# Second block's attention: the score product with the keys' low part over all 128 rows of the array

## The chip, the cores and the metric

The kernel runs on one core of a Trainium2 chip. Its engines are TensorE (PE, matrix products; its weight loader is shown apart as PEld), VectorE (DVE), ScalarE (ACT), GpSimd (POOL) and SyncE (SP, which issues most DMAs). The metric is the device time of one execution in microseconds, as the median of several runs.

## The reference, cut to what matters

The reference is a transformer of two blocks over 256 tokens of width 1024, in 32-bit floats. The first block (forgetting attention beside a convolution, cross attention to a memory, a mixture of experts) is not touched. The second block mixes a gated recurrence with a sparse attention (`nsa_mixer`), then follow a feed-forward layer and a per-layer embedding. In that attention, 16 query heads share 4 heads of keys and values (each key head serves 4 query heads, head width 64). It has a compressed branch, a branch over selected blocks and a window branch; at 256 tokens the last two see all earlier tokens:

```python
s = jnp.einsum('bgrqd,bgqkd->bgrqk', qr, kg)
o_sel = jnp.einsum('bgrqk,bgqkd->bgrqd', masked_softmax(s, m_sel), vg)
...
s = jnp.einsum('bgrqd,bgkd->bgrqk', qr, kwb)
o_win = jnp.einsum('bgrqk,bgkd->bgrqd', masked_softmax(s, m_win), vwb)
```

`qr` are the rotated queries, `kg` and `kwb` the rotated keys of the two branches. What is computed for both is the causal softmax of the scores, times the values.

## The kernel before

The kernel keeps its precision by splitting 32-bit numbers into a high part in the rounded type F32R and the low part that is left over. A product of two numbers is then made of high x high, high x low and low x high. The projections do this with three products for each 128 channels (`dense_nat`, `dense_T`); the weights' parts are made on ACT and DVE (`wsplit`, lines 182 and 183, tiles `wh` and `wl`) from chunks that SP loads ahead.

In the second block's attention a head has only 64 channels, half of the array's 128 rows. The kernel uses the other half for the low parts. Of the rotated queries (`qr`), a head's high part lies in its half of the partitions (lower half for even heads, upper for odd ones) and its low part in the other half. The rotated keys' high part (`kh`) and low part (`kl`) lie in both halves: ACT and DVE write one, POOL copies the other (lines 1461 and 1462). One product of `qr` with `kh` over all 128 rows so gives high x high and low x high at once.

Function `att` walks over the 16 heads in 18 steps. In a step stand the scores of a head, the transposes of the head before, and the products with the values of the one before that. The scores of a head are made in two tiles, one for each half of the queries (`hf`): the first with 2 x 128 columns (both branches, the first 128 keys), the second with 2 x 256. So there are 32 score tiles, 16 of 256 columns and 16 of 512. A tile is the sum of three products in one bank of PSUM: `qr` with `kh` (written `tr<-kh,qr` in the rows below, moving operand first), `qr` with `kl` (`tr<-kl,qr`), and the causal mask, an identity times a table of zeros and large negative numbers on the last 128 keys of each branch (`tr<-cnr,idr`, always 256 columns). Then come, for the softmax (`exps`), a maximum on DVE (line 318, `anm`) and two exponentials on ACT (line 322, `P`). Score tiles have two buffers (`tr`), so a tile's first product waits until ACT has read the tile before the last one.

PE takes its instructions in the order in which the scheduler of the language has put them. It mixes the attention's steps with the projections of the gates and the merge (`mm<-wh,xTh` and the like, 512 columns), so between the score tiles PE works on those, on transposes (`hp<-cs,P`, line 1505) and on the values' products (`po<-vt,PT`). All matmuls but the transposes are recorded under line 193, the helper `mm`; the rows are told apart by their tiles. The same instruction stands as LDWEIGHTS on PEld and as MATMUL on PE. `64*128` in a row means 64 rows and 128 columns of the array in use, and `128x512` the tile that is written. Another place with 64 rows is the compressed branch (`po<-VB,cPT`, 256 columns, in runs of four).

Of the kernel before, what the change touches and what calls it, by code (L numbers as in the profile page):

```python
# [9 lines left out]
F32R = mybir.dt.float32r  # L10
# [6 lines left out]
S = 256  # L17
D = 1024
EPS = 1e-6
NEG = -1e30  # L20
CAP = 32
# [17 lines left out]
def _consts():  # L39
# [20 lines left out]
    for L in LEVELS:  # L60
        b, r = p // L, p % L
        # columns in the blocks' right halves only
        m = (b[:, None] == b[None, :]) & (r[:, None] < max(L // 2, 1))
        lv.append(m[:, r >= L // 2])
# [71 lines left out]
class B:  # L136
# [31 lines left out]
    def wsplit(self, raw, kc, n):  # L168
        """F32R parts of a raw chunk: lists of per-k [128, n] views."""
# [25 lines left out]
    def dense_nat(self, xT, w, K, c0, n, evac, halves=2, ring=None):  # L195
        """[tok, n] products for columns c0..c0+n of w; evac(half, psum)."""
# [17 lines left out]
    def dense_T(self, xT, w, K, c0, n, starts, evac, cuts=(4, 4)):  # L214
        """[feature, tok] products for the 128-column windows `starts` of
        columns c0..c0+n of w; evac(i, psum [128, 256])."""
# [18 lines left out]
    def sq(self, src, acc, junk=None):  # L235
        """acc [128, 1] <- sum(src^2) / D over the free axis of [128, 512]."""
        return self.nc.scalar.activation(self.junk() if junk is None else junk, src, AF.Square, scale=1.0 / 32, accum_out=acc)

    def rfin(self, acc, r, eps=EPS):
        """r [128, 1] <- 1/sqrt(mean + eps) from the two sums of sq()."""  # L240
        ms = self.sm.tile([128, 1], F32, name="ms", bufs=4)
        self.nc.vector.tensor_scalar(ms, acc[:, 0:1], acc[:, 1:2], eps, op0=OP.add, op1=OP.add)
        return self.nc.gpsimd.tensor_tensor(r, ms, self.mhalf, op=OP.pow)

    def split_out(self, ps, hv, lv, g=None):
        """psum -> F32R parts, times a per-partition gain."""
# [6 lines left out]
    def parts(self, pool, C=8, tag=None):  # L253
        """Tiles for transposed F32R parts; k -> [128, S] of chunk k."""
# [5 lines left out]
    def norm_T(self, x, gk, out, n=D):  # L260
        """x: natural halves [128, n] -> x*g as [chan, tok] F32R parts."""
# [15 lines left out]
    def scaled(self, out, x, r, engines):  # L277
        """out <- x * r by halves of the columns; r: [128, 1]."""
# [9 lines left out]
    def tr_parts(self, nat, out, g=None, pool=None):  # L288
        """natural halves [128, D] -> transposed F32R parts."""
# [11 lines left out]
    # Sigmoids and the like go by way of tanh, which shares a table with exp.  # L301
    def sigmoid(self, out, x, hb=0.0):
        """out <- sigmoid(x + 2 hb)"""
# [3 lines left out]
    def silu2(self, out, x, t=None):  # L307
        """out <- 2 silu(x); t: scratch, if out may not be it."""
# [5 lines left out]
    def exps(self, sc, P, n, nm, sm, r=None):  # L314
        """sc: [128, heads, n] psum, times r; P <- exp(sc - max), sm <- row sums."""
# [10 lines left out]
    def build(self, upto=99):  # L326
        tc, nc, A = self.tc, self.nc, self.A
        with ExitStack() as ctx:
# [18 lines left out]
            # sums of squares and factors of the norms over X, by half  # L347
# [19 lines left out]
    def setup(self):  # L367
        """Constants that nothing waits for at the start."""
# [4 lines left out]
        # softmax over the two rows of logits: first row's share, and the rest  # L373
# [10 lines left out]
        # lb + (1 - lb) sigmoid(x) = lb' + lm' tanh(x / 2)  # L384
# [3 lines left out]
    def block1(self):  # L388
        tc, nc, A = self.tc, self.nc, self.A
        V = nc.vector  # L390
        with tc.tile_pool(name="sm1", bufs=1) as self.sm, tc.tile_pool(name="b1", bufs=1) as b1, \
# [28 lines left out]
            # conv gate and value, forget logits  # L420
# [22 lines left out]
            # depthwise causal conv  # L443
# [18 lines left out]
            # log forget gates and their running sum  # L462
# [11 lines left out]
            # q, k, v. The heads of a pair have their channels in different halves of the  # L474
            # partitions; the other half carries the gates: one-hot rows against -c, c against ones.
# [42 lines left out]
            # forgetting attention  # L518
# [33 lines left out]
            # memory keys and values; in between, layernorm + swish on the conv path  # L552
# [68 lines left out]
            # memory cross attention; the scores take the norm's factors  # L621
# [49 lines left out]
            # the residual goes to psum, too, where the experts add to it  # L671
# [26 lines left out]
    def first_max(self, name, *vals):  # L698
        """For each (value [128, .., n], onehots, maximum): onehots of the first position
        of the maximum over the last axis. The steps of the values alternate."""  # L700
# [20 lines left out]
    def busy(self, t, x, n, pool=None):  # L721
        """Products of t and x that nobody reads: they hold TensorE's clock up over a wait."""
# [6 lines left out]
    def logits(self, c, pool, pl):  # L729
        """Routing products of columns c*512.. of x, before the norm's factor."""  # L730
# [13 lines left out]
    def route(self, pool, pl, x):  # L744
# [4 lines left out]
        with self.urgent():  # L749
# [6 lines left out]
            for h in range(2):  # L756
# [4 lines left out]
                # the two largest of every group; then the group's  # L761
# [11 lines left out]
            # place of each token in its expert's list, from 1  # L773
# [6 lines left out]
            with tc.issue_after(last.ins):  # L780
                # number of the tokens beyond their expert's first CAP
                V.tensor_scalar(sel, pos, float(CAP) + 0.5, None, op0=OP.is_gt)
                # gates
# [5 lines left out]
                # the experts' table, while the engine waits  # L789
# [14 lines left out]
    def beyond(self, pool):  # L804
        """Number of the tokens beyond their expert's first CAP."""
# [9 lines left out]
    def onehots(self, q, P):  # L815
        """Tokens (rows) to places in the lists of four experts."""
# [6 lines left out]
    def moe_plan(self):  # L823
        """The experts' weight chunks in the order of their use, by fours."""
# [11 lines left out]
    def more(self, n):  # L836
        """Opens a pool of n more places for the experts' chunks."""
# [5 lines left out]
    def mload(self):  # L843
        """Loads the next chunk: rows of 512 for each of the four experts, or the last norm's gains."""
# [24 lines left out]
    def moe(self):  # L869
        """Four experts at a time, each with its places in its own quarter of the  # L870
        array's columns and of psum's partitions."""
# [4 lines left out]
        with tc.tile_pool(name="smm", bufs=1) as self.sm, tc.tile_pool(name="mo", bufs=1, reuse_waits="tile") as mo:  # L876
            T = lambda n, name: mo.tile([128, n], F32, name=name)
            with tc.tile_pool(name="pbig", bufs=2, space=PSUM) as pbig, \
# [3 lines left out]
                def gather(q, n=4):  # L882
                    """Inputs of the places, by channel, and the norm's factors for them."""
# [19 lines left out]
                def products(a, n, ps):  # L903
                    """ps <- products of n row blocks a(k) with as many weight rows, by expert."""
# [7 lines left out]
                def gates_t(q):  # L912
                    """Gates of the places, by token."""
# [66 lines left out]
                # this block's last norm and the next one's first: X <- x * g, with  # L980
                # the sums of squares of x and x * g
# [18 lines left out]
            with self.urgent():  # L1000
                for h in range(2):
                    # 1 / rms(x) and 1 / rms(x * g), the latter with eps * rms(x)^2 for eps
# [10 lines left out]
    def overflow(self, y, T, psm):  # L1013
        """Tokens beyond the first CAP of an expert: every expert over all tokens."""
# [4 lines left out]
        def load(ap):  # L1019
            # a queue of its own: those of the other loads need not come to rest  # L1020
            nc.gpsimd.dma_start(raw, ap)
            return raw

        with tc.If(n > 0):
            # by halves of the tokens; most of these are other tiles' places
# [34 lines left out]
    def rope(self, x, hf, H):  # L1060
        """Rotates the first 16 of each 64 of x [128, H*64] in place."""
# [12 lines left out]
    def post(self, m, ps, h, c, gb, acc):  # L1074
        """m <- psum * gain, and the sum of squares of the psum."""
# [4 lines left out]
    def post_add(self, m, h, acc, eps=EPS):  # L1080
        """X[:, h] += m / rms."""
# [8 lines left out]
    def block2(self):  # L1090
        tc = self.tc
        with tc.tile_pool(name="eo", bufs=1) as eo:
            # the recurrence's outputs, later the per-layer embedding
# [4 lines left out]
    def mixer(self, on):  # L1098
# [4 lines left out]
        with tc.tile_pool(name="sm2", bufs=1) as self.sm, tc.tile_pool(name="b2", bufs=1) as b2, \  # L1103
# [8 lines left out]
            # the recurrence's values go first and take the norm's factors themselves  # L1112
# [16 lines left out]
            with tc.tile_pool(name="s5", bufs=2) as s5p, tc.tile_pool(name="ap", bufs=1) as ap, \  # L1129
# [16 lines left out]
                # gated merge of the two branches  # L1146
# [59 lines left out]
    def hgrn(self, uT, W, on, hv, hg, php, other):  # L1206
        """The gated linear recurrence, two heads at a time; channels on partitions."""
# [3 lines left out]
        for b in range(4):  # L1211
# [12 lines left out]
            # products to fill the chain's waits with  # L1224
# [5 lines left out]
    def heads(self, fo, qq, hv, on, h0, tile, php):  # L1230
        """Two heads of the recurrence.
        Each pair (t, s) falls in one block of a binary tree over time, with s
        in its left and t in its right half: keys carry the decay up to the
        half's end, queries that from the half's start, both products of
        factors <= 1 that grow from level to level."""
# [9 lines left out]
        def pairs(q, L):  # L1245
            """Pairs of the blocks of L; their queries are the right halves."""
# [17 lines left out]
        while m < 128:  # L1264
            # tot: products of f over blocks of m
# [30 lines left out]
        # the queries' factor dk**-0.5 / 2 comes in here, and the output gates' half  # L1296
# [12 lines left out]
    def nsa(self, uT, W, s4, b2):  # L1309
# [3 lines left out]
        # compressed keys and values: transposed, second half of the partitions one token ahead  # L1313
# [14 lines left out]
        def compress():  # L1328
            """Keys and values at once: theirs are the lower and the upper half of the array's columns."""
# [21 lines left out]
            # twice the gelu  # L1351
# [20 lines left out]
        # queries, transposed in pairs of heads  # L1372
# [23 lines left out]
        # gates  # L1396
# [8 lines left out]
        # compressed branch  # L1405
# [33 lines left out]
        # rotated keys of both branches as parts, in both halves of the partitions; values  # L1439
# [24 lines left out]
        # rotated queries: a head's high part in its half of the partitions, the low one in the other  # L1464
# [10 lines left out]
        def att(ap, pax):  # L1475
            """Selected and window branches: causal over all keys at this length.
            Scores of a step, the transposes of the one before and the values'
            products of the one before that follow each other."""
            acc, Ps, PTs = {}, {}, {}

            def scores(h):
# [7 lines left out]
                rr = slice(64 * j, 64 * j + 64)  # L1489
                for hf, kb, c0 in ((0, 128, 0), (1, 256, 128)):  # L1490
# [3 lines left out]
                    self.mm(sc, q[rr], kl[g // 2][rr, g % 2, :, :kb], False, False)  # L1494
# [44 lines left out]
    def ffn(self, e):  # L1539
# [3 lines left out]
        with tc.tile_pool(name="smf", bufs=1) as self.sm, tc.tile_pool(name="ff", bufs=1) as ff, \  # L1543
# [4 lines left out]
            with tc.tile_pool(name="py2", bufs=1, space=PSUM) as py, \  # L1548
                    tc.tile_pool(name="pmm", bufs=4, space=PSUM) as self.pmm:
                self.ptr, self.trtag = self.pmm, "mm"  # L1550
                # With v = x r, relu(v W)^2 is r^2 relu(x W)^2: the norm over its product has
# [116 lines left out]
```

## Time and profile before

| | |
|---|---|
| time, median of 3 runs | 1365.17 us (1363.2 to 1365.42) |
| span of the profiled execution, from first to last instruction | 1360.5 us |
| PE busy in the span | 1205.7 us (89%) |
| DVE, ACT, POOL busy | 603.3, 486.5, 130.8 us |
| instructions | 17824, of them 7122 matmuls |
| the attention's 32 score tiles | from 979 to 1082 us of the span |
| DMA over the span | 332.38 MB, mean 244 GB/s |

The span is one profiled execution; the runs' time is a little longer, as it holds what lies before the first and behind the last instruction. An engine's busy share is a mean over stages with different limits. In the middle of the span, 300 to 740 us, the experts' weights stream in and DMA is busy all the time; at both ends PE is. PE counts as busy from a matmul's recorded start to its modelled end, and matmuls overlap: what a matmul really takes is read from one start to the next.

### The profile page before, as it was taken

The page shows a single profiled execution, that of the slowest core. Times are in us where ns is not written, and L with a number is a line of the kernel's source. Part 1 is how long each engine was busy: PE and PEld are TensorE (multiplying, and loading weights), DVE is VectorE, ACT ScalarE, POOL GpSimd, SP SyncE. Part 2 cuts the span into 40 slices and gives each one's busy share as a digit, 9 for nine tenths or more (in the row PEclk, how much of TensorE's full clock was granted, in tenths as well). Part 3 has the DMA queues.
Part 4 walks back from the last instruction along what each step waited for, and adds up shares of the span by engine and source line. Part 5 has one row for each costly group of instructions (what it writes and reads, how often), then busy time and mean ns, then how long its engine had stood idle before and what let it go on. Part 6 is the DMA issues. An engine that isn't in the chain of part 4 may idle for free.

```text
span 1360.5 us, 17824 instructions
## 1 busy us (share of the span) xinstructions
PE 1205.7 (89%) x7122; PEld 839.1 (62%) x7122; DVE 603.3 (44%) x1024; ACT 486.5 (36%) x923; POOL 130.8 (10%) x171
## 2 busy tenths in 40 slices
PE   8889999989676766676768999999999999999997
PEld 7779888733121212020302898888778888989886
DVE  5896655510000000000002678575756666565565
ACT  5677654300000000000003543244655446554553
POOL 3876000000000000000000000014100000000000
PEclk9989999989686978786867999999999999999999
DMA  8333695899999999999999554553522245565651
GB/s 291 112 128 119 236 374 195 277 372 381 387 385 388 388 390 386 390 386 390 387 390 350 161 170 133 159 169 117 164 91 76 85 157 178 186 195 179 202 199 47
DMA packets 174328, 332.38 MB, mean 244 GB/s; under 512 B 6368, under 2 KB 20512, under 8 KB 174240
## 3 DMA queue, kind: packets, MB, share of 16 engines
q1 hardware_dynamic: 173680, 329.87, 68.6%
q8 instruction: 58, 0.95, 0.3%
q10 hardware_dynamic: 560, 1.31, 0.3%
q14 instruction: 30, 0.25, 0.1%
HBM read 330.11 MB, written 1.05 MB: 243 GB/s over the span
## 4 chain that ended last, share of the span: by engine, by line
PE 51%; DMA 23%; SPq 2%; ACT 1%; DVE 1%; issue 1%; DVEq 0%; POOLq 0%; ACTq 0%
PE mm L193 29%; DMA w<-w_gate_in 7%; DMA w<-w_up_in 7%; PE z L193 7%; DMA w<-w_down_in 6%; PE bg L193 5%; PE po L193 2%; PE hp L193 2%; DMA wl<-w_up_in 2%; PE tr L193 2%; SPq L859 2%; PE sp L193 2%; PE hp L1505 1%; PE sp L960 0%; DMA w<-w_in_in 0%
## 5 line engine op out<-in xcount | busy, mean ns | idle before, releaser
L183 DVE TENSOR_TENSOR wl<-w,wh 128x1024 fp32r<-128x1024 f32 (+2 forms) x228 | 278.5, 1236 | 160.2 <-ACT wh L182 158.9
L182 ACT CAST wh<-w 128x1024 fp32r<-128x1024 f32 (+2 forms) x228 | 235.6, 1044 | 202.5 <-PE mm L193 161.0
L193 PE MATMUL bg<-w,xs 128*32 128x512 f32 x888 | 160.6, 827 | 72.8 <-DMA w<-w_up_in 35.4
L193 PE MATMUL mm<-xTh,wl 128*128 128x256 f32 x688 | 196.4, 290 | 11.3 <-DVE wl L183 11.1
L193 PE MATMUL mm<-xTh,wh 128*128 128x256 f32 x688 | 190.6, 290 | 5.5 <-ACT wh L182 2.8
L193 PE MATMUL mm<-xTl,wh 128*128 128x256 f32 x688 | 194.0, 288 | 0.2 <-DVE xTl L251 0.2
L193 PE MATMUL mm<-wl,xTh 128*128 128x512 f32 (+1 forms) x440 | 173.1, 396 | 0.3 <-DVE wl L183 0.3
L193 PE MATMUL mm<-wh,xTh 128*128 128x512 f32 (+1 forms) x440 | 168.5, 401 | 4.0 <-ACT wh L182 1.3
L193 PE MATMUL mm<-wh,xTl 128*128 128x512 f32 (+1 forms) x440 | 170.4, 395 | 0.0
L958 DVE SCALAR_TENSOR_TENSOR sg<-bg,rsl,sg 128x512 f32<-128x512 f32 x8 | 6.0, 751 | 343.8 <-PE bg L193 343.8
L193 PEld LDWEIGHTS bg<-w,xs 128*32 128x32 f32 x888 | 23.6, 125 | 198.0 <-DMA w<-w_up_in 80.5
L193 PEld LDWEIGHTS mm<-xTh,wl 128*128 128x128 f32 x688 | 133.1, 194 | 14.5 <-DVE wl L183 13.8
L193 PEld LDWEIGHTS mm<-xTh,wh 128*128 128x128 f32 x688 | 130.2, 194 | 8.1 <-ACT wh L182 3.5
L193 PEld LDWEIGHTS mm<-xTl,wh 128*128 128x128 f32 x688 | 132.5, 194 | 0.8 <-DVE xTl L251 0.4
L193 PEld LDWEIGHTS mm<-wh,xTh 128*128 128x128 f32 x440 | 82.4, 189 | 21.7 <-ACT wh L182 1.8
L193 PEld LDWEIGHTS mm<-wl,xTh 128*128 128x128 f32 x440 | 83.2, 189 | 18.0 <-DVE wl L183 1.9
L193 PEld LDWEIGHTS mm<-wh,xTl 128*128 128x128 f32 x440 | 83.0, 189 | 17.9 <-issue 0.7
L193 PE MATMUL bg<-w,ht 128*32 128x512 f32 x456 | 65.2, 663 | 25.1 <-DMA w<-w_down_in 24.3
L461 POOL TENSOR_TENSOR zc<-zc,zt 128x256 f32<-128x256 f32 x60 | 63.1, 1053 | 17.2 <-ACT zt L458 12.5
L977 ACT COPY od<-bg 128x512 f32<-128x512 f32 x16 | 9.4, 585 | 139.5 <-PE bg L193 134.7
L962 ACT COPY ht<-sp 128x512 f32<-128x512 f32 x8 | 4.7, 585 | 152.2 <-PE sp L960 152.2
L1243 POOL MEMSET At<- 128x512 f32 x4 | 2.0, 525 | 565.2 <-PE bg L193 458.2
(410 smaller groups left out, 1586.6 us busy)
## 6 DMA issues: line engine op xcount, KB each, us to landing
w<-w_down_in SPq DMA_DIRECT2D x73, 1024.0 KB, 14.4
w<-w_up_in SPq DMA_DIRECT2D x68, 1024.0 KB, 14.0
w<-w_gate_in SPq DMA_DIRECT2D x59, 1024.0 KB, 14.3
w<-w_in_in SPq DMA_DIRECT2D x41, 1024.0 KB, 5.2
w<-w_mkv_in SPq DMA_DIRECT2D x8, 1024.0 KB, 5.1
w<-w_out_in SPq DMA_DIRECT2D x8, 1024.0 KB, 5.1
wh<-w_up_in SPq DMA_DIRECT2D x12, 512.0 KB, 11.6
wl<-w_up_in SPq DMA_DIRECT2D x12, 512.0 KB, 11.4
```

The lines of the kernel that those rows point to most:

```text
L182: self.nc.scalar.copy(hv, raw[:, j:j + g, :])
L183: self.nc.vector.tensor_tensor(lv, raw[:, j:j + g, :], hv.bitcast(F32), op=OP.subtract)
L193: return self.nc.tensor.matmul(out, lhsT, rhs, start=start, stop=stop, skip_group_check=True)
L461: nc.gpsimd.tensor_tensor(zi, zi, t, op=OP.add)
L859: self.nc.sync.dma_start(a, src[:, j * n:(j + 1) * n])
L958: V.scalar_tensor_tensor(sg, ps, rsl[q], sg, op0=OP.mult, op1=OP.mult)
L962: nc.scalar.copy(ht, tp)
L977: nc.scalar.copy(od[q, c], ps)
L1243: nc.gpsimd.memset(At, 0.0)
L1505: nc.tensor.transpose(pt[:, b * 128:(b + 1) * 128], P[:, br, b * 128:(b + 1) * 128], idn)
```

## The change

In `scores`, the product with the keys' low part takes the whole of `qr` and `kl` and no longer the head's half `rr` of the partitions. It sums over 128 rows instead of 64 and adds the product low x low, which was left out before. The diff also empties comments and docstrings; without those it is:

```diff
@@ scores(h)
                 P = Ps[h] = ap.tile([128, 2, 384], F32, name="P", bufs=2)
-                rr = slice(64 * j, 64 * j + 64)
                 for hf, kb, c0 in ((0, 128, 0), (1, 256, 128)):
                     sc = self.ptr.tile([128, 2, kb], F32, name="tr")
                     q = qr[g][:, h % 4, hf * 128:(hf + 1) * 128]
                     self.mm(sc, q, kh[g // 2][:, g % 2, :, :kb], True, False)
-                    self.mm(sc, q[rr], kl[g // 2][rr, g % 2, :, :kb], False, False)
+                    self.mm(sc, q, kl[g // 2][:, g % 2, :, :kb], False, False)
                     self.mm(sc[:, :, kb - 128:], self.idr,
                             self.cnr[:, None, :].to_broadcast([128, 2, 128]), False, True)
```

The instructions stand in the same order on every engine, with line numbers one less behind the removed line. Two waits change places on PE. At the first score tile the rows are these, with before marked by - and now by +:

```order
 L193 MATMUL mm<-wh,xTh_4931 128x512
 L193 MATMUL tr<-kh,qr 128x256 [waits DVE_49,PE_49,Pool_49]
-L193 MATMUL tr<-kl,qr 128x256
+L193 MATMUL tr<-kl,qr 128x256 [waits Pool_49]
 L193 MATMUL tr<-cnr,idr 128x256
 L193 MATMUL tr<-kh,qr 128x512
```

The first product with `kl` now waits for POOL's copy of the low parts; in the third score tile, of the second head, where this wait stood, it is gone.

## Rows read from the trace of the kernel before

**Rows 1.** The page's first part: busy us (share of the span) xinstructions of each engine.

```profile
PE 1205.7 (89%) x7122; PEld 839.1 (62%) x7122; DVE 603.3 (44%) x1024; ACT 486.5 (36%) x923; POOL 130.8 (10%) x171
```

**Rows 2.** Busy time by window: window, us, engines (xcount), granted clock, DMA share, GB/s.

```profile
978.00:1082.00 104.00, 104.00 (x572) 81.82 (x570) 58.46 (x114) 55.77 (x165) 0.00 (x0) 1.00 0.27 92
...
1146.00:1150.00 4.00, 3.53 (x17) 3.56 (x18) 3.30 (x8) 3.90 (x11) 0.00 (x0) 0.57 0.67 245
```

**Rows 3.** The chain that ended last, from 960 to 1110: shares by line.

```profile
by line: PE mm L193 57.9%; PE tr L193 18.6%; PE po L193 13.4%; PE hp L1505 7.0%; PE tr L296 1.6%; PE mm L296 1.2%; PE tr L1385 0.6%
```

**Rows 4.** Waits from 975 to 1100: us in total, times, longest us.

```profile
DVE anm L318 <- PE tr L193: 31.4, 23, 4.3
```

**Rows 5.** Groups of weight loads, 978 to 1082: busy us, mean ns | idle before.

```profile
L193 PEld LDWEIGHTS tr<-kh,qr 128*128 128x128 f32 x32 | 6.1, 190 | 0.3
...
L193 PEld LDWEIGHTS tr<-cnr,idr 128*128 128x128 f32 x32 | 6.0, 186 | 5.9 <-issue 3.9
L193 PEld LDWEIGHTS tr<-kl,qr 64*128 64x128 f32 x32 | 5.8, 183 | 6.8 <-issue 5.6
```

**Rows 6.** Timeline of PE, a 512-column tile: start us, us, what.

```profile
986.70 0.47 PE L193 MATMUL tr<-kh,qr 128*128 128x512 f32 x1
987.10 0.50 PE L193 MATMUL tr<-kl,qr 64*128 64x512 f32 x1
987.53 0.39 PE L193 MATMUL tr<-cnr,idr 128*128 128x256 f32 x1
987.75 0.38 PE L1505 MATMUL hp<-cs,P 128*128 128x128 f32 x2
987.89 0.48 PE L193 MATMUL mm<-wl,xTh 128*128 128x512 f32 x1
988.21 0.40 PE L193 MATMUL mm<-wh,xTl 128*128 128x512 f32 x1
988.44 0.39 PE L193 MATMUL mm<-wh,xTh 128*128 128x512 f32 x1
```

**Rows 7.** Timeline of PEld, the same place.

```profile
987.10 0.18 PEld L193 LDWEIGHTS tr<-kl,qr 64*128 64x128 f32 x1 [0.24 <-issue]
987.53 0.19 PEld L193 LDWEIGHTS tr<-cnr,idr 128*128 128x128 f32 x1 [0.24 <-issue]
...
987.97 0.19 PEld L193 LDWEIGHTS mm<-wh,xTl 128*128 128x128 f32 x1
```

**Rows 8.** Timeline of PE, 256-column tiles behind values' products and behind a projection's.

```profile
992.50 0.36 PE L193 MATMUL tr<-kh,qr 128*128 128x256 f32 x1
992.79 0.38 PE L193 MATMUL tr<-kl,qr 64*128 64x256 f32 x1
...
998.63 0.28 PE L193 MATMUL tr<-kh,qr 128*128 128x256 f32 x1
998.84 0.38 PE L193 MATMUL tr<-kl,qr 64*128 64x256 f32 x1
999.15 0.38 PE L193 MATMUL tr<-cnr,idr 128*128 128x256 f32 x1
```

**Rows 9.** Timeline of PE, a run of 256-column products with 128 rows.

```profile
1150.08 0.28 PE L193 MATMUL mm<-xTl,wh 128*128 128x256 f32 x1
1150.20 0.28 PE L193 MATMUL mm<-xTh,wh 128*128 128x256 f32 x1
```

**Rows 10.** Timeline of PEld, a run of four 64-row products and what follows.

```profile
917.60 0.73 PEld L193 LDWEIGHTS po<-VB,cPT 64*128 64x128 f32 x4 [0.36 <-issue]
918.66 0.19 PEld L193 LDWEIGHTS mm<-wh,xTl 128*128 128x128 f32 x1 [0.33 <-issue]
```

**Rows 11.** Instructions on `kl`: ns min/median/max, first and last start us.

```profile
L1462 POOL CAST kl<-kl x8: 393/402/1391, 947.8 to 957.7; 64x256 fp32r<-64x256 f32 x8
```

**Rows 12.** Timelines of ACT and PE: a tile's last exponential, and the tile that takes its buffer.

```profile
1034.72 0.38 ACT L322 ACTIVATE P<-tr,anm 128x128 f32<-128x128 f32 x1
...
1035.76 0.36 PE L193 MATMUL tr<-kh,qr 128*128 128x256 f32 x1
```

## The prediction

> **What bounds the kernel now.** I read three things in this order: which engine is busy where the change sits, whether that engine waits there, and what its idle moments are.
>
> The page's first part says that TensorE (PE) is busy 89% of the span [rows 1]. A share over the whole span says little about one stage, so the second view is the busy time in the 104 us from 978 to 1082, in which all 32 score tiles of the second block's attention lie: PE is counted busy for all 104.00 us, VectorE (DVE) for 58.46 and ScalarE (ACT) for 55.77, the granted clock is 1.00 (the 2.4 GHz level) and the DMA engines are 27% busy [rows 2]. The chain that ended last runs from 960 to 1110 through PE alone: the shares of its PE groups add up to 100% [rows 3]. The list of waits agrees: DVE waits 31.4 us for the scores [rows 4], and no line of that list is one of PE's matmuls. So a microsecond less on PE here is a microsecond less at the end, as long as ACT and DVE keep up.
>
> A PE that counts as busy is not a PE at full rate, because the ends of matmuls are modelled. The third view is therefore the weight loader (PEld). Before its 32 loads for the high-part product the loader sits idle 0.3 us in all; before the 32 loads for the low-part product, which have 64 rows, 6.8 us; before the 32 loads for the mask, which follow them, 5.9 us [rows 5]. These 12.7 us are what the change is about.
>
> One score tile shows it. The three products of a 512-column tile start at 986.70, 987.10 and 987.53, and the next work at 987.75 [rows 6]: intervals of 0.40, 0.43 and 0.22. Three 512-column products in a row that all use 128 rows start at 987.89, 988.21 and 988.44 [rows 6]: 0.32 for the one that follows short transposes, then 0.23. The loader says why. The load for the product at 988.21 begins at 987.97, 0.24 ahead, while the product before it runs. The loads for the low-part product and the mask begin at 987.10 and 987.53, the moment their own products are recorded to start, each with 0.24 of idle loader before it [rows 7]. They are not done ahead: one load and the emptying of the array lie bare, once going from 128 rows to 64 and once coming back.
>
> Elsewhere in the kernel there are 64-row products too, in runs of four. There the loader idles 0.36 us before the four loads, not between them, and 0.33 us before the first 128-row load behind them [rows 10]. So it is the change of the row count that costs, not the 64 rows as such, and what follows may be an ordinary projection product: the mask's own form is not needed for it.
>
> **The change part by part.**
>
> Removed: 32 times the step from 128 to 64 rows and 32 times the step back. Working by tiles, from start to start:
> - 512 columns (16 tiles): now 0.40 + 0.43 + 0.22 = 1.05. Afterwards 0.32 for the high part (behind short work, as [rows 6] has it), 0.23 for the low part, and for the mask's 256 columns what 256 columns take in a run of 128-row products, 0.12 [rows 9]: 0.67. Saved 0.38.
> - 256 columns behind a projection product (7 tiles): now 0.21 + 0.31 [rows 8] and 0.22 for the mask, 0.74. Afterwards three times 0.12, 0.36. Saved 0.38.
> - 256 columns behind short work (9 tiles): now 0.29 for the first interval [rows 8], 0.82 in all. Afterwards 0.21 (0.12, and 0.09 for the bare load, as 0.32 stands to 0.23), 0.12 and 0.12. Saved 0.37.
>
> Sum: 16 x 0.38 + 7 x 0.38 + 9 x 0.37 = 12.1 us. The cruder second way is the loader's idle time, 6.8 + 5.9 = 12.7 us [rows 5]. I take the middle, 12.4.
>
> Added: the low-part product sums over 64 more rows. Columns set how long a product streams, and these stay; a 128-row product of the same 512 columns takes 0.23 [rows 6], already in the sum. The weight loads stay 32 in number; those with 64 rows take no less time than those with 128 (5.8 us busy against 6.1 in [rows 5]). So the cost is zero, and the bound is that of the mask's interval, the one of which no row shows it behind a 128-row product of this kind: 0.12 at best, 0.22 if nothing changes there, that is 32 x 0.10 = 3.2 us less gain. I take 0.12, since [rows 10] puts the same gap before a plain product. A price below zero is excluded: the same columns still stream.
>
> Here the Trainium skill speaks against the change. Its page "TensorE: Matmul & The Clock Gate" (Part 3, The mechanism) says that a weight load overlaps with matmuls in flight "only when row_grp differs"; by that rule the new loads, which use all rows like the product before them, would lie as bare as now, and the sum would be zero. [rows 7] contradict it for this chip: a 128-row load runs 0.24 ahead under a 128-row product. By the trace the sum stays 12.4.
>
> Moved: nothing but one wait. Every engine's instructions stand in the same order; the first low-part product now waits for GpSimd (POOL), since it reads both copies of the keys' low part, and the third score tile, which did so before, no longer does. Behind the waiting instruction stands all of PE, but POOL's last copy of the low parts starts at 957.7 and the longest takes 1391 ns [rows 11]; the product comes behind 979, where the score tiles begin, some 20 us later. Cost nothing; cover 20 us. No DMA and no queue is passed.
>
> Where the time goes next: PE stays the last engine. A tile's buffer comes back from ACT, and the closest call that I found is the tile at 1035.76, whose buffer ACT had released at 1034.72 + 0.38 = 1035.10, 0.66 us ahead [rows 12]. A tile gains 0.38, and ACT's work is fed by PE and moves with it, so I count no new wait; the price if I am wrong in this crowded place (four tiles between 1030 and 1041) is 4 x 0.38 = 1.5 us. After the attention everything to the end hangs on PE and moves as a block. One loose term is there: from 1146 to 1150, behind the norm, the mean granted clock is 0.57 [rows 2], mostly the 1.2 GHz level. If the block lies differently against such a stretch, up to 1.5 us may come or go (4 us at about half rate, with PE in part waiting).
>
> The profile's span is 1360.5, the median of the runs 1365.17, so 4.7 us lie around the span. Span after: 1360.5 - 12.4 = 1348.1; time 1352.8.
>
> **The rivals.**
> - The mask's gap stays: its load is late for a reason of its own (a repeated operand, the same bank of PSUM) and not because rows change. For it: no row shows the mask behind a 128-row product of the new kind. Against it: [rows 10]. Only the idle before the low-part loads goes, 6.8: 1358.4.
> - The gain turns into waits for the softmax: PE reaches a tile whose buffer or exponentials aren't there. For it: 0.66 us at 1035.76 [rows 12]. Against it: ACT and DVE are busy little over half of the stretch [rows 2], and DVE waits for PE's scores [rows 4]. 1.5 us in the crowded place gives 1354.3; as much again elsewhere, 1355.8.
> - The change doesn't do what it says: the loads stay bare since all products of a tile share rows (the rule above), or they have to wait for something that isn't the row count. 1365.2. Against it: [rows 7, 10].
> - Slower: the 64-row product now runs beside its neighbours on the idle half of the array, and the change takes that away. Then 16 passes of 0.23 and 16 of 0.12 come on top, 5.6 us: 1370.8. It decides from the point at which a low-part product costs less than a full pass now. Against it: it costs 0.43 where a full pass takes 0.23 [rows 6]. The Trainium skill's page "TensorEngine Tiling (Array Packing)" (Overview, Theoretical Speedup) promises up to 2x for 64 rows; here no second 64-row product stands next to it, and the trace shows no gain.
>
> **How the numbers follow.** Forecast 1352.8, with waits of up to 1.5 us and the clock's 1.5 us in it: 82%. Mask's gap or more waits, 1356 to 1360: 10%. Nothing: 5%. Slower: 3%. The range: down to 1350.0 (12.7 gained, 1.5 of clock, 1 for the spread of runs, which lay between 1363.2 and 1365.4), up to 1357.5 (3.2 less for the mask and 1.5 of waits). About 0.2%, 2.7 us, is what a measurement can tell from no change: faster than 1362.4 takes the first two cases, 92%; within 5%; slower 3%.
>
> **What would show it.** In the trace after, the loader's idle time before the low-part and mask loads falls from 12.7 us to under 2; a 512-column tile's intervals read 0.32, 0.23 and 0.12; the 32 tiles end about 12 us earlier counted from the first; DVE waits less for the scores; no new wait of PE between 978 and 1090. If the mask's load still starts with its product, the first rival holds. If PE's list of waits names ACT, the second. I am wrong altogether if the low-part intervals stay at 0.43 and 0.31.

## The result, and the profile after

The changed kernel took 1348.26 us (median of 4 runs, 1347.07 to 1349.01), the kernel before, in the same session, 1364.49 (4 runs): ratio 0.9892, 95% interval 0.988 to 0.9904. It is faster by 16.2 us. The forecast was 1352.8, with a range down to 1350.0; the measured time lies 1.7 us below that end. The profiled execution has a span of 1347.3 and a time of 1348.96.

The page's first part: busy us (share of the span) xinstructions of each engine. It answers [rows 1].

```profile
PE 1192.2 (88%) x7122; PEld 838.0 (62%) x7122; DVE 603.8 (45%) x1024; ACT 486.3 (36%) x923; POOL 130.1 (10%) x171
```

PE does as many instructions and is busy 13.5 us less; ACT, DVE and POOL do what they did. Where it went is seen in the loader. The groups of weight loads of the score tiles (busy us, mean ns | idle time of the loader before them), which answer [rows 5]:

```profile
L193 PEld LDWEIGHTS tr<-kl,qr 128*128 128x128 f32 x32 | 6.1, 191 | 0.3
L193 PEld LDWEIGHTS tr<-kh,qr 128*128 128x128 f32 x32 | 6.1, 190 | 0.4
L193 PEld LDWEIGHTS tr<-cnr,idr 128*128 128x128 f32 x32 | 6.0, 188 | 0.7
```

The idle time before the low-part and the mask loads fell from 12.7 us to 1.0. The loads themselves last as long as before.

One 512-column tile on PE (start us, us, what), answering [rows 6]:

```profile
986.25 0.47 PE L193 MATMUL tr<-kh,qr 128*128 128x512 f32 x1
986.56 0.39 PE L193 MATMUL tr<-kl,qr 128*128 128x512 f32 x1
986.79 0.28 PE L193 MATMUL tr<-cnr,idr 128*128 128x256 f32 x1
986.91 0.38 PE L1504 MATMUL hp<-cs,P 128*128 128x128 f32 x2
```

and its loads on PEld, answering [rows 7]:

```profile
986.33 0.19 PEld L193 LDWEIGHTS tr<-kl,qr 128*128 128x128 f32 x1
986.56 0.19 PEld L193 LDWEIGHTS tr<-cnr,idr 128*128 128x128 f32 x1
```

From start to start it is 0.31, 0.23 and 0.12 where it was 0.40, 0.43 and 0.22. The loads now run 0.23 ahead of their products, under the product before. The two kinds of 256-column tiles, behind values' products and behind a projection's, answer [rows 8]:

```profile
991.65 0.36 PE L193 MATMUL tr<-kh,qr 128*128 128x256 f32 x1
991.86 0.28 PE L193 MATMUL tr<-kl,qr 128*128 128x256 f32 x1
991.97 0.28 PE L193 MATMUL tr<-cnr,idr 128*128 128x256 f32 x1
...
996.99 0.28 PE L193 MATMUL tr<-kh,qr 128*128 128x256 f32 x1
997.11 0.28 PE L193 MATMUL tr<-kl,qr 128*128 128x256 f32 x1
997.23 0.28 PE L193 MATMUL tr<-cnr,idr 128*128 128x256 f32 x1
```

Summed over all 32 tiles, from the first product's start to that of the instruction behind the mask, the tiles take 17.03 us where they took 29.51: 12.48 less. The whole attention, from the first score product to the last product with the values, went from 110.3 us (979.0 to 1089.3) to 97.8 (979.7 to 1077.5).

Nothing took the place of what was removed. The list of PE's waits from 960 to 1100 is empty, the chain in that stretch still runs through PE alone, and DVE waits less for the scores than in [rows 4] (us in total, times, longest):

```profile
DVE anm L318 <- PE tr L193: 20.1, 15, 3.9
```

### The profile page after: what moved, and what is told of

Same layout as the page of the kernel before. It is cut to its first block, busy times and chain, and to the rows that moved or that the text cites. A ratio compares the mean times of both kernels' runs of the same rounds, so it can differ in the third digit from the quotient of the medians.

```text
span 1347.3 us, 17824 instructions
## 1 busy us (share of the span) xinstructions
PE 1192.2 (88%) x7122; PEld 838.0 (62%) x7122; DVE 603.8 (45%) x1024; ACT 486.3 (36%) x923; POOL 130.1 (10%) x171
## 4 chain that ended last, share of the span: by engine, by line
PE 51%; DMA 24%; SPq 2%; DVE 1%; ACT 1%; issue 1%; DVEq 0%; POOLq 0%; ACTq 0%
PE mm L193 29%; DMA w<-w_up_in 8%; DMA w<-w_down_in 8%; PE z L193 7%; DMA w<-w_gate_in 6%; PE bg L193 5%; PE po L193 3%; PE hp L193 3%; SPq L859 2%; DMA wl<-w_up_in 1%; PE sp L193 1%; PE tr L193 1%; PE hp L1504 1%; PE sp L960 0%; DVE sg L958 0%
## 5 line engine op out<-in xcount | busy, mean ns | idle before, releaser
L193 PEld LDWEIGHTS mm<-xTh,wl 128*128 128x128 f32 x688 | 132.5, 193 | 13.9 <-DVE wl L183 13.3
```

What stands on the lines that cost most here:

```text
L193: return self.nc.tensor.matmul(out, lhsT, rhs, start=start, stop=stop, skip_group_check=True)
```

## The experiments

Twelve runs, in three sessions on different chips. Each session has its own runs of the kernel before.

**Is the difference that of the kernels?** First a copy of each, unchanged.

> The kernel before once more, unchanged. What is open: between the two medians lie 16.2 us, in the attention of the two traces 12.5. Theory 1: the rest is not the change's, but the place where the low clock happens to fall and how the experts' loads go in an execution. Then the 32 tiles again take 29.5 us from their first products to the next work, the time is within 0.2% of before, but other stretches of the trace (0 to 980, 1082 to the end) differ from the trace shown before by 1 to 3 us, and the stretch of low clock behind the norm (1146 to 1150) may be absent. Theory 2: the rest belongs to the change (something behind the attention got faster). Then the stretches outside the attention agree with the trace before within 0.5 us, low clock behind the norm included.

Measured: 1361.76 us (11 runs), ratio to the kernel before 0.9994 (0.9985 to 1.0003). So there is no difference between two copies. But the runs of the kernel before alone, 15 of them, lie between 1360.32 and 1364.49. Taken by itself, this copy's trace reads as theory 2 wanted: outside the attention its stages lie within 0.5 us of those of the first trace, and the low clock behind the norm is there again (0.94 in the window from 1125 to 1155 in both).

> The changed kernel once more, unchanged. Theory 1: the tiles take 17.0 us again, 12.5 less; the whole time comes out 12.5 to 16 us below the kernel before in the same rounds, and the stretches outside the attention differ from those of the first trace of it by 1 to 3 us; the low clock behind the norm may appear. Theory 2: a difference of 16 us again, and never a low clock behind the norm.

Measured: 1349.58 us (4 runs, 1348.53 to 1352.31) beside 1362.07, ratio 0.9904 (0.9889 to 0.9919): 12.5 us less, not 16.2. The 32 tiles take 17.03 us and the attention 97.8, as in the first trace. The low clock behind the norm, which theory 2 ruled out for this kernel, is there (0.94 in the same window).

**Half of it: 128 rows in the 512-column tiles alone.**

```diff
-                    self.mm(sc, q, kl[g // 2][:, g % 2, :, :kb], False, False)
+                    if hf:
+                        self.mm(sc, q, kl[g // 2][:, g % 2, :, :kb], False, False)
+                    else:
+                        self.mm(sc, q[rr], kl[g // 2][rr, g % 2, :, :kb], False, False)
```

> 128 rows for the low-part product of the 512-column tiles alone, 64 rows in the 256-column tiles as before. Theory 1, each pair of row changes costs 0.39 us whatever the tile's size: the 512-column tiles take 0.665 us each, the others 0.74 or 0.83 as before, together 17.0/2 and 29.5/2, about 23.2 us; 6.3 us less than before in the attention. Rival (the gain comes from the array's rows being used more fully, so it grows with columns): two thirds of 12.5, 8.3 us.

Measured: 1356.36 us (4 runs), ratio 0.9949 (0.9934 to 0.9965). The tiles take 23.24 us and the attention 104.0 (979.5 to 1083.5): 6.3 us of the 12.5, from half of the tiles. The loader's groups, the two kinds of tiles apart:

```profile
L193 PEld LDWEIGHTS tr<-cnr,idr 128*128 128x128 f32 x32 | 6.0, 187 | 2.7
L193 PEld LDWEIGHTS tr<-kl,qr 128*128 128x128 f32 x16 | 3.1, 192 | 0.0
L193 PEld LDWEIGHTS tr<-kl,qr 64*128 64x128 f32 x16 | 2.9, 183 | 2.9 <-issue 1.7
```

The loads with 128 rows lie under the product before, those with 64 don't, in one and the same kernel. 512 columns bring no more than 256: the price is one of the excursion to 64 rows and back, not of what streams.

**Who pays for the way back?** The kernel before, with the 64-row product moved behind the mask, so that the mask now stands behind a 128-row product and something else follows the 64 rows.

```diff
                     self.mm(sc, q, kh[g // 2][:, g % 2, :, :kb], True, False)
-                    self.mm(sc, q[rr], kl[g // 2][rr, g % 2, :, :kb], False, False)
                     self.mm(sc[:, :, kb - 128:], self.idr,
-                            self.cnr[:, None, :].to_broadcast([128, 2, 128]), False, True)
+                            self.cnr[:, None, :].to_broadcast([128, 2, 128]), False, False)
+                    self.mm(sc, q[rr], kl[g // 2][rr, g % 2, :, :kb], False, True)
```

> The kernel before with the 64-row product moved behind the mask: high part, mask, low part. The number of row changes is the same. Theory 1: the mask's load is now made ahead (idle before it under 1 us in all), the low-part loads stay bare (6 to 7 us idle), and the bare load behind them moves to whatever comes next (transposes, projections); the 32 tiles together with the first instruction behind them cost the same, so the attention is within 1 us of before. Rival (the mask's gap is its own): the mask keeps about 6 us of idle loader before it, and the next work behind the tile shows none.

Measured: 1362.92 us (one run); attention 109.3 us (980.7 to 1090.0), 1.0 less. The loader's groups, with the transposes `hp<-cs,P` that now often follow:

```profile
L1505 PEld LDWEIGHTS hp<-cs,P 128*128 128x128 f32 x90 | 10.9, 144 | 5.7 <-issue 3.6
...
L193 PEld LDWEIGHTS tr<-cnr,idr 128*128 128x128 f32 x32 | 6.1, 191 | 0.3
L193 PEld LDWEIGHTS tr<-kl,qr 64*128 64x128 f32 x32 | 5.8, 183 | 6.1 <-issue 4.0
```

Behind a 128-row product the mask's load waits 0.3 us in all, where it waited 5.9 [rows 5]. The idle time has not gone: it stands before the transposes, 5.7 us where the copy of the kernel before has 1.5, and before the projections' loads, 8.9 us where it has 7.2. The mask's form (a repeated operand, the same bank) was not the cause; whoever comes first behind 64 rows pays. The 1.0 us may come from the transposes' shorter load, 144 ns to the mask's 186.

**Is it each 64-row product, or the run of them?** The kernel before, with its 64-row product cut in two, one for each branch.

```diff
-                    self.mm(sc, q[rr], kl[g // 2][rr, g % 2, :, :kb], False, False)
+                    for br in range(2):
+                        self.mm(sc[:, br, :], q[rr], kl[g // 2][rr, g % 2, br, :kb], False, False)
```

> The kernel before, with its 64-row product split in two, one for each branch: two 64-row products of half the columns behind each other, so twice as many 64-row products and as many row changes as before. Theory 1, the price hangs on the change of rows: no bare load between the two (loader idle before the low-part loads still 6 to 7 us for 64 loads instead of 32), the attention within 1.5 us of before (110.3 us from the first score product to the last values' product). Rival (each 64-row product costs its 0.39 us): 12 us more, about 122 us.

Measured: 1364.47 us (one run); attention 111.0 us (982.1 to 1093.1), 0.7 more.

```profile
L193 PEld LDWEIGHTS tr<-kl,qr 64*128 64x128 f32 x64 | 9.4, 185 | 6.9 <-issue 5.7
...
L193 PEld LDWEIGHTS tr<-cnr,idr 128*128 128x128 f32 x32 | 6.0, 186 | 3.3
```

Twice as many 64-row loads leave the loader idle for the same 6.9 us. In a 512-column tile the intervals are 0.40, 0.43 for both halves together, and 0.22, as with one product (the idle time before the mask reads less, 3.3 us, since the second half's load fills a part of the same interval). So the switch costs, once per way, and a run of 64-row products pays it once.

**The same cure in another place.** The runs of four 64-row products in the compressed branch [rows 10] pay too. First, in the changed kernel, two products with the values block-diagonal over 128 rows in place of four (marked `...`: how the values' tile is filled, and two transposes of 128 columns in place of four of 64).

```diff
...
-                self.mm(po[:, r].rearrange("p g d -> p (g d)"), PT[:, 2 * r2 + r, :],
-                        VB.rearrange("p g d -> p (g d)"), True, True)
+                self.mm(po.rearrange("p r g d -> p (r g d)"), PT[:, r2, :],
+                        VB.rearrange("p r g d -> p (r g d)"), True, True)
```

> The changed kernel, and the same thought at the compressed branch: the values of two heads of a group stand block-diagonal in 128 rows, so that one product of 128 rows and 512 columns takes the place of two of 64 rows and 256 columns, and two transposes of 128 columns that of four of 64. The four runs of 64-row products and the two of 64-column transposes go. By theory 1 each of the four runs cost 0.39 us and the transposes' change of columns about as much: 1.6 to 2.4 us less than the changed kernel, between the first product of the recurrence and the first score tile (189.4 us in the traces so far, then 187 to 188); that puts it 14 to 15 us below before. Rival (TensorE waits there for other engines, or POOL's extra fill and copy are late): no difference to the changed kernel, or up to 1 us more.

Measured: 1351.09 us (6 runs, 1348.05 to 1354.56), ratio to before 0.9923 (0.991 to 0.9936). The gain missed; the stretch from the recurrence's first product to the feed-forward's first one is 1.2 us longer than in the changed kernel (345.7 to 344.5). Where the change was made it did its work: from the product before a run to the second one behind it, PE needs 1.32 us in each of the first two runs, where it needed 1.72. (The time to the next instruction alone, 2.22 us for all four runs against 4.23, says too much: in three of them the next product is recorded as starting 0.03 us behind the last one.) But with fewer instructions the scheduler ordered PE's work anew, score tiles come some 11 us earlier, and PE waits where it didn't. Two lines of its waits from 1075 to 1160, both new:

```profile
PE tr L296 <- DVE xTl L249: 0.8, 1, 0.8
PE mm L193 <- ACT xTh L249: 0.7, 1, 0.7
```

These are 1.5 us of what was given back; the rest is spread and was not followed.

Hence a second try that keeps the order: four products as now, each over 128 rows, 64 of them zeros.

```diff
...
-                nc.tensor.transpose(pt[:, r, :], P2[:, r].rearrange("p g n -> p (g n)"), idn)
+                r0 = min(r, 2)
+                nc.tensor.transpose(pt[:, r, :], P2[:, r0:r0 + 2].rearrange("p r g n -> p (r g n)"), idn)
...
-                            VB.rearrange("p g d -> p (g d)"), True, True)
+                            VB[:, (2 * r2 + r) // 3].rearrange("p g d -> p (g d)"), True, True)
```

> The changed kernel, and in the compressed branch the four transposes take 128 columns instead of 64 and the four products with the values 128 rows instead of 64 (64 of them zero; the output stays the reference's). TensorE's instructions stand in exactly the changed kernel's order, other than in the kernel with block-diagonal values, whose order shifted. Now a run of four such products takes 1.06 us to the next instruction, four times in the kernel, 4.23 us in all. Theory (the change of the row count costs, twice per run, wherever it stands): four passes of 0.12 and a bare load of 0.09 behind short work, 0.48 to 0.57 a run, 2.0 to 2.3 us in all, so 1.9 to 2.2 us less; total time 0 to 3 us below the copies of the changed kernel, the scatter being as large as the gain. Rival (what cost there was the load of P's transpose or the late bank, not the rows): 1.06 us a run as now, 4.2 us in all.

Measured: 1349.05 us (4 runs), ratio to before 0.9909 (0.9895 to 0.9923), not to be told from the two copies of the changed kernel beside it (1347.81 and 1348.2). In the trace the recurrence stage, up to the first score product, lasts 188.2 us; in five traces of the changed kernel 189.2 to 189.8. Its loader, the group of all 16 loads, and the first run with the load behind it, to be held against [rows 10]:

```profile
L193 PEld LDWEIGHTS po<-VB,cPT 128*128 128x128 f32 x16 | 2.9, 190 | 0.4
```

```profile
917.57 0.85 PEld L193 LDWEIGHTS po<-VB,cPT 128*128 128x128 f32 x4
918.45 0.19 PEld L193 LDWEIGHTS mm<-wh,xTl 128*128 128x128 f32 x1
```

The gap of 0.36 before the run and that of 0.33 behind it are gone. From the product before the run to the second one behind it PE needs 1.32 us instead of 1.72: 0.40 less in two of the four runs, 0.34 in the other two, 1.5 us in all. The expectation of 1.9 to 2.2 less was too high, as it took 0.12 for each pass; here 256 columns take 0.22 from start to start, with 64 rows and with 128. Nor does the other term of the expectation for the block-diagonal kernel, a price for the transposes' change of columns, show: the loader idles 0.3 us before the eight transposes `tr<-cs,cP` in both traces, with 64 columns and with 128. The price of a switch there and back is the same as in the score tiles, where it is 12.48 / 32 = 0.39.

**Then what are the other microseconds?** Copies of both kernels again, in two more sessions.

> The changed kernel a third time. Theory 1: attention 97.8 us; 12 to 13 us below the kernel before of the same rounds; what is beyond that comes from the experts' stage and the low clock behind the norm, which one execution in several lacks. Theory 2: 16 us below before in the same rounds.

Measured: 1347.64 us (4 runs) beside 1361.19 (11 runs): 13.6 less, ratio 0.9906 (0.9892 to 0.9921), a little more than the 12 to 13 of theory 1. Attention 97.8.

> The kernel before, one more look, for the stretches outside the attention. Theory 1: attention 110.3 us; experts' stage 472 to 474 us; feed-forward stage 181.4 us with the low clock behind the norm or 179.8 without. Theory 2: the feed-forward stage always has it in the kernel before.

Measured: 1363.74 us (one run). Attention 110.3. The low clock behind the norm is absent in this trace and the feed-forward stage lasts 179.9 us, against theory 2.

> The changed kernel once more, beside a run of the kernel before. So far it lay 16.2, 12.5 and 13.6 us below, while the attention took 12.5 us less in every trace. Theory: the change is worth 12.5 us, and what goes beyond is the scatter of executions of either kernel (beginning, experts, low clock behind the norm). Then the attention lasts 97.8 us from the first high-part score product to the last values' product, and the runs of this copy and the next, taken together, lie 11 to 14.5 below the runs of the kernel before. Rival: the first session told the true size, and 16 us come back here, with 3.7 us in some other stage of the changed kernel that is shorter in all of its traces.

Measured: 1347.81 us (4 runs) beside 1361.72 (11 runs): 13.9 less, ratio 0.9897 (0.9883 to 0.9911). Attention 97.8.

> A second copy of the changed kernel on the same chip, for the scatter between builds of one and the same kernel. Theory: within 1.5 us of the copy before it; attention 97.8 us; beginning 264 to 271 us, experts 471 to 475 us with no order in it. Rival: as there, 16 us below the kernel before in both copies.

Measured: 1348.2 us (6 runs, 1347.55 to 1352.85): 13.5 less, ratio 0.9907 (0.9893 to 0.9921). Attention 97.8.

> The kernel before once more, for one more trace of it: attention 110.3 us, sum of the 32 score tiles 29.5 us. Theory: its other stages lie within what the traces of the changed kernel show. Rival: its beginning or its experts are longer than in every trace of the changed kernel.

Measured: 1362.82 us (one run). Attention 110.3.

The attention's length is told by the first score product and the last product with the values. The two rows of a tile view (ns min/median/max, first and last start) of the copies in the first of these two sessions, first of the kernel before:

```profile
L193 PE MATMUL po<-vt,PT x192: 217/275/276, 995.2 to 1092.3; 128*128 128x64 f32 x192
```

```profile
L193 PE MATMUL tr<-kh,qr x32: 279/382/482, 982.0 to 1083.3; 128*128 128x256 f32 x16, 128*128 128x512 f32 x16
```

and of the changed one:

```profile
L193 PE MATMUL po<-vt,PT x192: 218/275/276, 987.6 to 1073.8; 128*128 128x64 f32 x192
```

```profile
L193 PE MATMUL tr<-kh,qr x32: 278/378/481, 976.0 to 1065.2; 128*128 128x256 f32 x16, 128*128 128x512 f32 x16
```

982.0 to 1092.3 is 110.3 us, 976.0 to 1073.8 is 97.8. Here the attention starts 6 us earlier in the changed kernel, in others of its traces later than in the kernel before. The stages of four traces of the kernel before and five of the changed one:

| stage | before, 4 traces | changed, 5 traces |
|---|---|---|
| start to the experts | 266.6 to 268.6 | 264.8 to 268.7 |
| experts | 471.7 to 474.1 | 471.8 to 473.9 |
| from there to the recurrence | 50.1 | 50.1 |
| recurrence to first score | 189.2 to 189.9 | 189.2 to 189.8 |
| attention | 110.3 | 97.8 |
| from there to the feed-forward | 57.1 to 57.2 | 57.2 |
| feed-forward | 179.9 to 181.4 | 179.8 to 181.4 |
| from there to the end | 32.7 | 32.7 |
| span | 1360.5 to 1362.0 | 1345.1 to 1350.6 |

Only the attention is apart; every other stage of the one kernel overlaps with that of the other. The rival, that another stage is shorter too, has no stage to stand on.

## Why the prediction was right or wrong

**What bounds the kernel, and the mechanism: right.** The loader's idle time fell from 12.7 us to 1.0 (forecast: under 2), and the two runs that move the cost, `e_last` and `d_two`, show that it belongs to the change of the row count and not to the mask or to each 64-row product. The prediction put the price down to a bare load and the emptying of the array. The two loads alone last 183 and 186 ns [rows 5], 0.37 of the 0.39 us per tile; what the emptying adds to them, no run separates.

**The sum: right.** 12.48 us measured, 12.4 taken, 12.1 by tiles. That it fits to 0.1 us is partly luck: 12.4 is the middle of two ways that lie 0.6 apart. By kind: 512 columns 0.67 a tile as forecast; 256 columns behind a projection 0.36; behind short work 0.44, forecast 0.45. The added rows cost nothing: 0.23 for 512 columns.

**The mask's gap stays, 1358.4: refuted.** 0.7 us of idle loader before its loads.

**Waits for the softmax: refuted.** No wait of PE between 960 and 1100. DVE still waits 20.1 us for the scores: PE is still the last engine there.

**Loads stay bare, 1365.2: refuted.** The low-part loads run 0.23 ahead of their products. The sentence of the Trainium skill's page "TensorE: Matmul & The Clock Gate" (Part 3, The mechanism) that lets a load overlap only when the row group differs is contradicted by the low-part and the mask loads, whose products use all rows like the ones before them. The same section also lets a load run ahead when it goes to the background weight buffer, so the prediction's rival followed one sentence of it and not the whole; which buffer these loads go to, no run shows. The Trainium skill's page "TensorEngine Tiling (Array Packing)" (Key Properties) says that changing the tiling mode drains TensorE; with that the trace agrees, in that a load at a change of the row count isn't made ahead, at 0.39 us there and back.

**Slower by lost concurrency, 1370.8: refuted** by the 0.43 that became 0.23.

**The time: wrong, by the step from the span to the runs.** The prediction read 1360.5 of span against a median of 1365.17 and concluded that "4.7 us lie around the span". In every execution whose span and time are both known, of either kernel, 1.6 to 1.8 us do: here 1348.96 - 1347.3 = 1.7. The other 3 us were not around the span. The time of the execution profiled before isn't on record, but with 1.7 around its span it comes to 1362.2, below the quickest of the three timed runs (1363.2): the sum set the span of one execution against the median of others that took longer. With 1.7 the same sum gives 1360.5 + 1.7 - 12.4 = 1349.8, and the measured 1348.26 is then 1.5 us away, inside the scatter of the copies (medians 1347.64 to 1349.58); the range's low end, moved by the same 3 us, would have been 1347.0. Added to the median of the runs, the sum started from a high draw: the kernel before took 1364.49 in that session and 1361.19 to 1362.07 in all others.

**The spread: too small.** The low end held 1 us for it. Single runs of the kernel before lie between 1359.67 and 1365.42, those of the changed kernel between 1346.77 and 1352.85, and a median of three or four runs moves by 1 to 3 us with them. That is also why the gain came out as 16.2, 12.5, 13.6, 13.9 and 13.5 us.

**The clock term: right in size, wrong in kind.** The prediction held 1.5 us for a stretch of low clock behind the norm that the moved block might meet or miss. The clock does make these 1.5 us, but in either kernel. Windows of the 30 us around (us, engines, granted clock, DMA share, GB/s), first two executions of the kernel before, then two of the changed one:

```profile
1125.00:1155.00 30.00, 27.96 (x152) 24.13 (x151) 20.18 (x34) 20.48 (x39) 1.11 (x2) 0.94 0.59 202
```

```profile
1125.00:1155.00 30.00, 27.96 (x154) 23.66 (x154) 19.98 (x33) 19.47 (x38) 1.10 (x2) 1.00 0.59 205
```

```profile
1125.00:1155.00 30.00, 27.69 (x206) 26.04 (x205) 21.62 (x40) 20.17 (x39) 1.10 (x2) 1.00 0.58 193
```

```profile
1125.00:1155.00 30.00, 27.68 (x188) 25.79 (x187) 21.35 (x39) 19.41 (x41) 1.11 (x2) 0.94 0.60 202
```

Where the clock is 0.94 in that window, a part of it is at the 1.2 GHz level, and the feed-forward stage lasts 181.3 to 181.4 us; where it is 1.00, 179.8 to 179.9. Three of four traces of the kernel before have it, three of five of the changed one. The first profile after happened to lack it.

**What stays open.** All sessions lie at 12.5 or above. Over all runs the medians are 1361.9 (54 runs of the kernel before and its copies) and 1348.35 (22 runs), 13.6 apart, 1.1 more than the attention explains. The mean spans of the traces, 1361.2 and 1348.1, are 13.1 apart. No stage of the traces shows the rest; whether it is scatter or a small effect outside of the attention isn't settled.

## What to carry to other kernels

A lone product over half of the rows between full ones is not half the price: it pays for the way to 64 rows and back, 0.39 us here, which is more than the 0.23 us of a full 512-column pass. Fill the rows (with a term that is left out otherwise, or with zeros) or put the half-row products together in a run, and look whether the scheduler keeps its order. When a sum is made against one profiled execution, add to it only what lies around that execution's span, and take the scatter of the runs from more than three of them.

## What the runs showed of the hardware

- A switch from 128 rows to 64 and back costs 0.34 to 0.40 us in two places of the kernel at the 2.4 GHz level, whether 256 or 512 columns stream and whether one, two or four products stand between. In the score tiles the lower half of the rows (even heads) and the upper half (odd heads) cost the same. The two loads that lie bare make up nearly all of it (183 and 186 ns). No run tries a switch to another number of rows.
- A 256-column product of the compressed branch takes 0.22 us from start to start, one of the score tiles 0.12 behind another product with all rows. The former's operands are plain 32-bit floats, the latter's the rounded F32R; whether that makes the difference wasn't tried.
- In the nine traces of the two kernels the scatter lies in the first 270 us (264.8 to 268.7), the experts (471.7 to 474.1) and the low clock behind the norm (1.5 us), while the attention has the same length to 0.1 us in every trace of a kernel.
